# A hybrid attention/recurrence block on one core: VectorE, ScalarE and SP of the recurrence ordered by hand with a clock per engine

## The chip, the core and the metric

The kernel runs on one core of a Trainium2 chip. A core has a matrix engine (TensorE, PE in the profile; its weight loads are PEld), three elementwise engines (VectorE or DVE, ScalarE or ACT, GpSimd or POOL), a queue engine that issues transfers (SyncE or SP) and 16 DMA engines. Each engine takes its own instructions in a fixed order and waits at the head of that order for semaphores of the others. The metric is the device time of one execution in microseconds, as the median of several.

## What is computed

One block on 1024 tokens of width 1024, in float32. A projection of the normalized and modulated input feeds three branches: attention with a forget gate (8 heads of 64), a linear recurrence with a low-rank state update (RWKV-7, 8 heads of 64), and two sigmoid gates that mix the two. A feed-forward part with a short convolution follows. The recurrence, which the change is about:

```python
def step(state, inp):
    r_t, w_t, k_t, v_t, a_t, b_t = inp
    sa = jnp.einsum('bhvk,bhk->bhv', state, a_t)
    state = state * w_t[:, :, None, :] + sa[..., None] * b_t[:, :, None, :] + v_t[..., None] * k_t[:, :, None, :]
    y_t = jnp.einsum('bhvk,bhk->bhv', state, r_t)
    return state, y_t
_, y = lax.scan(step, state0, (tm(r_h), tm(w_h), tm(k_h), tm(v_h), tm(a_vec), tm(b_vec)))
```

Its output is normalized over each head, gets a bonus term `sum(r*k*r_k) * v`, and is multiplied by a gate.

## The kernel before

**Split products.** A float32 product is made from three products of rounded halves: an operand `x` is cast to `hi` (ScalarE) and `lo = x - hi` (VectorE), and PE adds `hi*hi + hi*lo + lo*hi`. So a tile of the projection (128 columns of `w_in`, one half of 512 tokens) is 24 matmuls into one PSUM bank, and each weight tile has a transfer on SP, a cast on ScalarE (line 272) and two subtractions on VectorE (line 274).

**Stages.** First the norms and the low-rank inputs, then the low-rank products (`lora_chain`), then the recurrence, attention, the branch and output products, and the feed-forward part. The stages overlap through one mechanism, the class `Weave`.

**Weave.** It keeps one number, `now`, an estimate of PE's time in ns, which every matmul advances by `mm_cost`. Python generators called chains emit instructions and yield the time that they want to wait. `run` always resumes the chain with the smallest rank whose time has come, and when none is due, `fill` emits matmuls from a queue of large tiles until one is: the tiles of q and k (`qk_steps`), of r, k, v of the recurrence (`rkv_items`), of the attention's v (`v_steps`) and of the 16 gates (`gate_steps`). So PE's order is written out by hand, chains and fill interleaved. The order on the other engines is not: the framework orders VectorE, ScalarE, GpSimd and SP in this stage with its own simulated timeline. What the recurrence has not used of the fill is run in attention, where a late form of the gates (`late_gate`, PSUM bank `rk_ps`) fills PE.

**The recurrence** works on 8 units: 4 pairs of heads times 2 halves of the sequence. A unit has 8 chunks of 64 tokens, and two heads side by side on the partitions. `pre_chain` runs `pre` for one unit after the other, `main_chain` runs `main` behind it.

- `pre` loads the decay and `a` (`cum`, `al`), scans, takes exponentials, normalizes the key (`head_sums`, line 686: a sum over each head as a product with a block matrix, of a high and a low half; the low half is a GpSimd subtraction, line 689), and makes the scaled operands `ar` and `bk`. PE forms their products per chunk (`p`, masked into `E` on line 758). The 32x32 diagonal blocks of `E` go through DRAM to another layout (`sm`, then `M32`; lines 766 and 770), 31 rows of an inverse are made there by pairs of small VectorE instructions (lines 778 and 780, 62 per unit), and the result returns through DRAM (`se`, then `TT`; lines 783 and 791). Meanwhile transposes (`vt`, `at`, `tb`) and a product `q` fill `UV`, `QA` and the third part of `E`.
- `main` completes the inverse (`X`, `xi`, `zi`), makes `Wt`, `Zt`, `Mt` and the parts of state and output that need no earlier state (`sp`, `yp`), and then steps through the chunks: a product of `Mt` and the state into `sp` and a scaling on VectorE into the next state `S` (line 897). Then comes the output: two more head sums (`mu`, `va`), the norm, the bonus and the gate.

**Waits in the order.** The points at which chains yield are fixed times found for this kernel (1150 ns between state steps, 2000 to 3400 ns at other places, 38500 ns for the inverse). The PSUM pool `gen` has four banks for the chains, `big` two for the fill.

**q, k and the heads of attention.** Each half tile of q or k is split and stored by six transfers of 64 rows into `d_st`, which holds for every head the stacked operands that attention multiplies (line 399). `load_head` (line 988) fetches a head by three GpSimd transfers, `stA`, `stB` and `vh`.

Of the kernel before, what the change touches and what calls it, by code (L numbers as in the profile page):

```python
# [9 lines left out]
F32 = mybir.dt.float32  # L10
# [6 lines left out]
S = 1024  # L17
# [26 lines left out]
NCST = _n  # L44
NC1 = 384
# [3 lines left out]
class Weave:  # L49
# [3 lines left out]
    def __init__(self):  # L53
        self.now = 0.0
        self.first = deque()
        self.queue = deque()
        self.cur = None
        self.loaded = deque()
        self.hold = 0.0
        self.clock = {}  # L60
        self.late = 0

# [22 lines left out]
    def step(self):  # L85

        while True:
            if self.cur is None:
# [4 lines left out]
                self.cur = run(w)  # L93
                self.prefetch()
            if next(self.cur, self) is not self:
                return True
            self.cur = None

# [14 lines left out]
    def spawn(self, chain, wait=0.0):  # L113

        self.live.append([self.now + wait, 0, chain])

    def run(self, chains):

        self.live = [[self.now, 1 + i, g] for i, g in enumerate(chains)]
        while self.live:  # L120
# [7 lines left out]
            else:  # L128
                due[0] = self.now + max(wait, 0.0)


@with_exitstack
def hybrid_block(ctx: ExitStack, tc: tile.TileContext, a, out):
# [70 lines left out]
    d_st = dr.tile([8, 4, 128, S], F32R, name="d_st")  # L204
# [50 lines left out]

    def load_w(src, name, pool=None, n=1024, scale=None, tags=("whi", "wlo"), bufs=2):

        pool = pool or wp
        raw = rp.tile([128, n], F32, tag="raw", name=f"raw_{name}")
# [5 lines left out]
        if weave.late == 1:  # L265
# [4 lines left out]
            weave.spawn(lower(9000), 0)  # L270
        else:
            nc.scalar.copy(hi, raw)  # L272
            for c in range(0, n, NH):
                nc.vector.tensor_tensor(lo[:, c : c + NH], raw[:, c : c + NH], f32(hi[:, c : c + NH]), op=ALU.subtract)  # L274
        return hi, lo
# [50 lines left out]

    def gate_steps(w, i, pps, ptag, pool, tag):
        if weave.late == 1:
            yield from late_gate(w, i)
            return  # L330
        for hf in range(2):
            cs = slice(hf * NH, hf * NH + NH)
            ps = pps.tile([128, NH], F32, tag=ptag, name=f"gt{i}_{hf}")
            yield from gemm_steps(ps, w, u, cs)

# [10 lines left out]
    with ExitStack() as es:  # L346
# [4 lines left out]
        def big(name):  # L351
            return pb.tile([128, NH], F32, tag="big", name=name)
# [4 lines left out]
        def shifted(w, ti, hf, dst, prev, name, by_kt=False):  # L357

            ps = big(f"ps_{name}{hf}")
            yield from gemm_steps(ps, w, u, slice(hf * NH, hf * NH + NH), by_kt=by_kt)  # L360
            sh = shp.tile([128, NH + 1], F32, tag="sh", name=f"sh_{name}{hf}")
# [7 lines left out]
            stt(dst, ps, omu[:, ti : ti + 1], sh[:, 0:NH], op0=ALU.mult, op1=ALU.add)  # L369

        rkv, got, last_col = {}, {}, {}

        def rkv_items(p, hf):
# [3 lines left out]
            def steps(w, x, t):  # L377
                if hf == 0:
                    last_col[p, x] = shp.tile([128, 1], F32, tag=f"pv{x}", name=f"pv{p}{x}")
                yield from shifted(w, t, hf, ts_[x], last_col[p, x], f"rkv{t}")  # L380
                got[p, hf] += 1
# [3 lines left out]

        def qk_steps(w, i):
            sc_ = 0.125 if i < 4 else 1.0
            for hf in range(2):
                cs = slice(hf * NH, hf * NH + NH)
                ps = big(f"qk{i}_{hf}")  # L390
                yield from gemm_steps(ps, w, u, cs)
                hi = gsp.tile([128, NH], F32R, tag="sp0", name=f"qh{i}_{hf}")
# [3 lines left out]
                h0 = 2 * (i % 4)  # L396
                for t, k, r0 in ((hi, 0, 0), (lo, 0, 64), (hi, 2, 0)) if i < 4 else ((hi, 1, 0), (hi, 1, 64), (lo, 3, 0)):
                    for h in range(2):
                        nc.sync.dma_start(f32(d_st[h0 + h, k, r0 : r0 + 64, cs]), f32(t[h * 64 : h * 64 + 64, :]))
# [157 lines left out]
        with tc.tile_pool(name="lg", bufs=1, reuse_waits="tile") as lg, \  # L557
# [65 lines left out]
            def forget():  # L623
# [10 lines left out]
                for hf in range(2):  # L634
# [28 lines left out]
                    nc.sync.dma_start(f32(d_st[:, 2, 64:68, cs]), f32(r[:, 0:4, :]))  # L663
                    nc.sync.dma_start(f32(d_st[:, 3, 64:68, cs]), f32(r[:, 2:6, :]))
# [21 lines left out]
        def head_sums(ps, x, hi, lo):  # L686

            nc.scalar.copy(hi, x)
# [1294 lines left out]
```

## Time and profile before

| | us |
|---|---|
| median of 3 runs (1680.43 to 1682.48) | 1680.87 |
| the profiled execution's own time | 1681.63 |
| its span in the trace | 1679.9 |
| granted TensorE clock, mean of the span | 0.993 |
| VectorE busy in the span | 1219.1 |
| ScalarE busy in the span | 806.3 |
| GpSimd busy in the span | 131.2 |

Views of the trace are read as follows. A row of a group names line, engine, operation, output and inputs by tile, shapes and count, then busy time and mean ns of one, then the idle time before them and what ended it. A row of waits names the waiting engine and tile, who released it, and total, number and longest. A row of the timeline begins with the start in us from the span's start and the length; in brackets stands the idle time before it. The window rows give busy time of every engine in a stretch. All matmuls have line 141 and all transposes line 145, since a helper records them, so they are told apart by tile. The end of a matmul is modelled, so the busy time of PE contains some waiting.

### The profile page before, as it was taken

The numbers are of one execution on the slowest core, as the hardware profiler recorded it, in microseconds if no ns is written. First come the engines' busy times: TensorE is split into PE (matmuls) and PEld (weight loads), VectorE is DVE, ScalarE is ACT, GpSimd is POOL, SyncE is SP. The second block draws the span as 40 slices with busy tenths as digits, with TensorE's granted clock in tenths as the row PEclk, the third lists the DMA queues.
The fourth block names the chain that finished last, engine by engine and source line by source line (L and its number), as shares of the span: only waits on it lengthen the run. The fifth ranks groups of instructions, "written<-read, shape, count | busy, mean of one in ns | idle before, by whom it ended". The sixth has DMA issues, their size and how long they took to land.

```text
span 1679.9 us, 26265 instructions
## 1 busy us (share of the span) xinstructions
PE 1630.3 (97%) x9870; PEld 1344.6 (80%) x9870; DVE 1219.1 (73%) x2402; ACT 806.3 (48%) x1481; POOL 131.2 (8%) x151
## 2 busy tenths in 40 slices
PE   7999999999999999999999999999999999999998
PEld 7777777787877778888878888888888888888886
DVE  5786787878866635888778455897777777786677
ACT  5563334434445446676633243654444444455455
POOL 0011001111111011212022000000000000000000
PEclk9999999999999999999999999999999999999999
DMA  8487644443332228434197420133322323584463
GB/s 332 143 322 233 181 124 123 130 120 98 100 112 88 89 67 202 126 108 128 35 335 262 177 88 38 63 120 111 109 95 94 119 95 107 182 276 152 130 211 108
DMA packets 121503, 240.79 MB, mean 143 GB/s; under 512 B 40032, under 2 KB 48608, under 8 KB 121376
## 3 DMA queue, kind: packets, MB, share of 16 engines
q1 hardware_dynamic: 112896, 220.74, 40.2%
q0 software_dynamic: 8480, 18.37, 4.3%
q8 instruction: 78, 1.28, 0.3%
q14 instruction: 49, 0.40, 0.1%
HBM read 173.51 MB, written 65.54 MB: 142 GB/s over the span
## 4 chain that ended last, share of the span: by engine, by line
PE 74%; DVE 14%; DMA 5%; ACT 3%; issue 2%; SPq 1%; DVEq 0%; ACTq 0%
PE X L141 13%; PE D L141 12%; PE Y L141 6%; PE wo L141 5%; PE ps_rkv L141 5%; PE br L141 5%; PE gt L141 4%; PE W L141 3%; PE rk_ps L141 3%; PE qk L141 2%; PE lg L141 2%; PE ov L141 2%; DVE E L780 2%; DVE t L778 2%; PE tr L141 2%
## 5 line engine op out<-in xcount | busy, mean ns | idle before, releaser
L141 PE MATMUL D<-op,op 128*128 128x512 f32 x924 | 209.8, 389 | 0.0
L141 PEld LDWEIGHTS D<-op,op 128*128 128x128 f32 x924 | 173.3, 188 | 36.3 <-DVE op L1246 0.3
L141 PE MATMUL X<-T_m,S 128*128 128x512 f32 x440 | 107.2, 390 | 0.2 <-ACT x L1522 0.2
L141 PEld LDWEIGHTS X<-T_m,S 128*128 128x128 f32 x440 | 82.4, 188 | 18.3 <-ACT x L1522 0.6
L1245 ACT CAST op<-g 128x512 fp32r<-128x512 f32 x77 | 47.8, 621 | 73.7 <-PE D L141 48.5
L1246 DVE TENSOR_TENSOR op<-g,op 128x512 fp32r<-128x512 f32 x77 | 53.0, 688 | 41.4 <-ACT op L1245 41.1
L1482 DVE SCALAR_TENSOR_TENSOR c<-ab,vec,c 128x512 f32<-128x512 f32 x88 | 65.9, 749 | 19.5 <-ACT c L1485 17.9
L778 DVE TENSOR_TENSOR t<-E,M 128x60 f32<-128x60 f32 (+24 forms) x248 | 57.6, 232 | 25.7 <-DMA M<-sm 20.3
L1446 DVE TENSOR_TENSOR S<-ur,S 128x512 fp32r<-128x512 f32 x66 | 45.5, 691 | 35.9 <-ACT S L1442 35.8
L1442 ACT CAST S<-ur 128x512 fp32r<-128x512 f32 x66 | 41.0, 622 | 55.8 <-DVE ur L1435 30.6
L1446 DVE TENSOR_TENSOR A<-ur,A 128x512 fp32r<-128x512 f32 x64 | 44.0, 688 | 30.9 <-ACT A L1442 30.7
L274 DVE TENSOR_TENSOR lo_in<-raw_in,hi_in 128x512 fp32r<-128x512 f32 x84 | 56.5, 712 | 12.5 <-PE gt L141 4.6
L141 PE MATMUL Y<-T_h,A 128*128 128x512 f32 x264 | 63.4, 389 | 0.0
L141 PE MATMUL Y<-T_h,S 128*128 128x512 f32 x264 | 63.3, 389 | 0.0
L272 ACT CAST hi_in<-raw_in 128x1024 fp32r<-128x1024 f32 x42 | 43.8, 1047 | 40.1 <-PE ps_rkv L141 23.2
L1048 ACT ACTIVATE P<-lg,nm 128x896 f32<-128x896 f32 (+3 forms) x64 | 47.5, 743 | 29.0 <-DVE nm L1044 20.8
L141 PE MATMUL X<-B_b,A 128*128 128x512 f32 x252 | 60.8, 390 | 0.0
L141 PE MATMUL W<-B_f,A 128*128 128x512 f32 x252 | 60.6, 389 | 0.0
L780 DVE TENSOR_TENSOR E<-E,t 128x60 f32<-128x60 f32 (+24 forms) x248 | 54.9, 221 | 5.7
L141 PEld LDWEIGHTS Y<-T_h,A 128*128 128x128 f32 x264 | 49.5, 188 | 10.4
L141 PEld LDWEIGHTS Y<-T_h,S 128*128 128x128 f32 x264 | 49.5, 188 | 10.3
L1442 ACT CAST A<-ur 128x512 fp32r<-128x512 f32 x64 | 39.9, 623 | 34.1 <-PE X L141 29.4
(475 smaller groups left out, 4130.9 us busy)
## 6 DMA issues: line engine op xcount, KB each, us to landing
raw_in<-in_w_in SPq DMA_DIRECT2D x50, 512.0 KB, 3.9
wm<-in_w_mod SPq DMA_DIRECT2D x48, 512.0 KB, 7.2
ur<-in_w_up SPq DMA_DIRECT2D x44, 512.0 KB, 4.2
g<-d_g SPq DMA_DIRECT2D x35, 512.0 KB, 4.1
d_g<-gs SPq DMA_DIRECT2D x44, 256.0 KB, 2.0
d_g<-c SPq DMA_DIRECT2D x33, 256.0 KB, 4.4
d_st<-qh SPq DMA_DIRECT2D x64, 128.0 KB, 2.4
stA<-d_st POOLq DMA_DIRECT2D x8, 1024.0 KB, 6.4
```

Source lines behind the costliest of these rows:

```text
L141: nc.tensor.matmul(o, lhsT, rhs, start=start, stop=stop, skip_group_check=more)
L272: nc.scalar.copy(hi, raw)
L274: nc.vector.tensor_tensor(lo[:, c : c + NH], raw[:, c : c + NH], f32(hi[:, c : c + NH]), op=ALU.subtract)
L778: tt(tv, E32[:, 0:J, s : s + 1].to_broadcast([128, J, W]), M32[:, s : s + 1, s + 1 : 32].to_broadcast([128, J, W]), op=ALU.mult)
L780: tt(E32[:, 0:J, s + 1 : 32], E32[:, 0:J, s + 1 : 32], tv, op=ALU.add)
L1048: nc.scalar.activation(e[:, 0:n], lg[:, 0:n], AF.Exp, bias=nm[:, 0:1], accum_out=nm[:, 1:2])
L1245: nc.scalar.copy(hi, src)
L1246: tt(lo, src, f32(hi), op=ALU.subtract)
L1442: nc.scalar.copy(hi, src)
L1446: tt(lo, src, f32(hi), op=ALU.subtract)
L1482: stt(c, ab[:, x + hf * NH : x + hf * NH + NH], V("conv_w", 22 * x + i), c, op0=ALU.mult, op1=ALU.add)
```

## The change

- In the recurrence VectorE, ScalarE and SP are put under the hand-made order as well: their instructions run in the order in which the program emits them.
- `Weave.on` is a clock for each engine. A chain asks for an engine with a cost in ns and a time from which its input is there, waits until the engine would be at most 250 ns from free, and gets the time at which the result is there (200 ns are added for the semaphore, 350 ns for a PSUM bank to drain, and 85 ns are taken off for the overlap of two instructions). All fixed waits of `pre` and `main` are replaced by such times.
- The fill's evacuations and weight splits become chains of their own (`evacuate`, `split_w`), spawned with rank 0 and 0.5. `room` and `ready_w` emit them at once where a bank or a weight is needed.
- The inverse rows become a chain (`solve`) of rank 1.5: behind `main` (1), ahead of `pre` (2).
- The four PSUM banks of the chains are handed out by `take` and `give`.
- The low halves of the head sums are VectorE subtractions (`halves_of`) and no longer on GpSimd.
- q and k are stored by kind (`d_qk`: q or k, high or low, 512 rows of all heads), two transfers of 128 rows per half tile. The forget sums go to `d_f`. `load_head` gathers a head by six transfers of 64 rows, two of four rows, and one for v.
- PE's cost model has other figures while the recurrence runs, among them 95 ns for a change between large and small matmuls.
- `run` ends with the two main chains and then emits what is left of the spawned ones; tiles beyond 12 left in the queue, if there are any, are run then, ahead of `load_head(0)`.

The core of the diff:

```diff
+LATENCY = 200.0
+DRAIN = 350.0
+OVERLAP = {"DVE": 85.0, "ACT": 85.0}
+AHEAD = 250.0
...
+    def on(self, engine, cost, after=0.0, ahead=AHEAD):
+        while not self.force:
+            wait = max(self.clock.get(engine, 0.0), after) - ahead - self.now
+            if wait <= 0:
+                break
+            yield wait
+        start = max(self.clock.get(engine, 0.0), after, self.now)
+        self.clock[engine] = start + cost - OVERLAP.get(engine, 0.0)
+        return start + cost + LATENCY
+
+    def through(self, chain):
+        self.force += 1
+        for _ in chain:
+            pass
+        self.force -= 1
...
+        if self.timed:
+            small = lhsT.shape[0] <= 64 or m <= 64
+            if small != self.small:
+                self.small = small
+                self.now += 95
+            if lhsT.dtype == F32R:
+                self.now += n / 2.2
+            else:
+                self.now += max(n, 50) * (0.87 if small else 1.74)
+            return
...
+    def split_w(hi, lo, raw, i):
+        while weave.worked < i - 1 and not weave.force:
+            yield 200
+        t = yield from weave.on("ACT", 1050)
+        nc.scalar.copy(hi, raw)
+        yield t - weave.now
+        for c in range(0, 1024, NH):
+            yield from weave.on("DVE", 700, t)
+            tt(lo[:, c : c + NH], raw[:, c : c + NH], f32(hi[:, c : c + NH]), op=ALU.subtract)
...
+    def room():
+        while len(outs) > 1:
+            weave.through(outs.popleft())
+
+    def evacuate(chain):
+        outs.append(chain)
+        weave.spawn(chain, DRAIN)
...
-                h0 = 2 * (i % 4)
-                for t, k, r0 in ((hi, 0, 0), (lo, 0, 64), (hi, 2, 0)) if i < 4 else ((hi, 1, 0), (hi, 1, 64), (lo, 3, 0)):
-                    for h in range(2):
-                        nc.sync.dma_start(f32(d_st[h0 + h, k, r0 : r0 + 64, cs]), f32(t[h * 64 : h * 64 + 64, :]))
+                for x, t in enumerate((hi, lo)):
+                    nc.sync.dma_start(f32(d_qk[i // 4][x][i % 4 * 128 : i % 4 * 128 + 128, cs]), f32(t))
...
-        def head_sums(ps, x, hi, lo):
-            nc.scalar.copy(hi, x)
-            nc.gpsimd.tensor_tensor(lo, x, f32(hi), op=ALU.subtract)
-            yield 3400
+        def halves_of(x, hi, lo, after=0.0):
+            t = yield from act(620, after)
+            nc.scalar.copy(hi, x)
+            t = yield from dve(690, t)
+            tt(lo, x, f32(hi), op=ALU.subtract)
+            return t
+
+        def head_sums(name, hi, lo, after):
+            yield after - weave.now
+            yield from take(1)
+            ps = gen(name)
             mm(ps, blk_r, hi, start=True, stop=False)
             mm(ps, blk_r, lo, start=False, stop=True)
+            return ps, weave.now + DRAIN
...
+        def solve(o, n, E, after):
+            sm = scr.tile([2, NCU, 2, 32, 32], F32, tag="sm", name=f"sm{n}")
...
+            after = t + 1800
+            while turn:
+                yield 200
+            turn.append(n)
...
+            after = t + 3500
+            t32 = rw.tile([128, 256], F32, tag="t32", name=f"t32{n}", bufs=1)
+            for s in range(31):
+                J, W = s // 4 + 1, 31 - s
+                tv = t32[:, 0 : J * W].rearrange("p (j w) -> p j w", w=W)
+                t = yield from weave.on("DVE", 220, after)
+                tt(tv, E32[:, 0:J, s : s + 1].to_broadcast([128, J, W]),
+                   M32[:, s : s + 1, s + 1 : 32].to_broadcast([128, J, W]), op=ALU.mult)
+                t = yield from weave.on("DVE", 220, t - LATENCY)
+                tt(E32[:, 0:J, s + 1 : 32], E32[:, 0:J, s + 1 : 32], tv, op=ALU.add)
+                after = t - LATENCY
...
+            o["ready"] = t + 2800
...
             for c in range(last_c + 1):
                 if S[c] is not None:
+                    yield t - weave.now
                     for h in range(2):
                         mm(sp[HS[h], c, :], Mt[HS[h], c, :], S[c][HS[h], :], start=False, stop=c == last_c, more=True)
                 S.append(rw.tile([128, CH], F32, tag="state", name=f"S{n}{c}", bufs=9))
-                marks["S"] = ts(S[-1], sp[:, c, :], pcd[:, c : c + 1], None, op0=ALU.mult)
-                if c + 1 < NCU:
-                    yield 1150
+                t = yield from dve(280, weave.now + DRAIN)
+                ts(S[-1], sp[:, c, :], pcd[:, c : c + 1], None, op0=ALU.mult)
...
-        weave.run([main_chain(), pre_chain()])
+        with tc.manual_schedule(engines={mybir.EngineType.SP, mybir.EngineType.DVE, mybir.EngineType.Activation}):
+            weave.timed = True
+            weave.run([main_chain(), pre_chain()])
+            while len(weave.queue) > 12:
+                weave.step()
+            weave.finish()
+            for x in (*outs, *splits):
+                weave.through(x)
+            weave.timed = False
...
-        nc.gpsimd.dma_start(A, d_st[h, 0:2, :, :].rearrange("k r s -> r k s"))
-        nc.gpsimd.dma_start(B[0:68, :, :], d_st[h, 2:4, 0:68, :].rearrange("k r s -> r k s"))
+        hs = slice(h * 64, h * 64 + 64)
+        for t, rs, k, x in ((A, 0, 0, 0), (A, 0, 1, 0), (A, 64, 0, 1), (A, 64, 1, 0), (B, 0, 0, 0), (B, 0, 1, 1)):
+            nc.gpsimd.dma_start(t[rs : rs + 64, k, :], d_qk[k][x][hs, :])
+        for k in range(2):
+            nc.gpsimd.dma_start(B[64:68, k, :], d_f[h, 2 * k : 2 * k + 4, :])
```

`take(n)` yields until n of the four `gen` banks are given back and then until the latest of their times; `give(t)` returns a bank as free from t.

More of the change, by code (lines that the diff above doesn't have):

```diff
@@ L684, in hybrid_block, with take, give, dve @@
         nc.gpsimd.dma_start(blk_r, a["cst"][:, NC2 : NC2 + 128].bitcast(F32R))
-        def head_sums(ps, x, hi, lo):
-            nc.scalar.copy(hi, x)
-            nc.gpsimd.tensor_tensor(lo, x, f32(hi), op=ALU.subtract)
-            yield 3400
+        free = deque([0.0] * 4)
+        def take(n):
+            while len(free) < n:
+                yield 100
+            yield max(free.popleft() for _ in range(n)) - weave.now
+        def give(t):
+            free.append(t)
+        def dve(cost, after=0.0):
+            return weave.on("DVE", cost, after)
@@ L750, in pre @@
             UV = chunk_tile("UV", 2, NCU, 2, CH)
+            made = []
             for c0 in range(0, NCU, 4):
+                yield from take(2)
                 ps = [gen(f"p1_{n}{h}{c0}") for h in range(2)]
@@ L795, in pre @@
+            rkb = tmp("ksq")
+            t_rkb = yield from dve(745)
+            stt(rkb, rr, V("r_k", p), al, op0=ALU.mult, op1=ALU.mult)
+            yield from take(2)
             vt, at = gen(f"vt{n}"), gen(f"at{n}")
```

381 lines of the change are left out of this document (275 added, 106 removed).

## The prediction

> **What bounds the kernel now.** The page gives the profiled execution's span, the busy shares, and the count of engines that could be the limit.
>
> ```profile
> span 1679.9 us, 26265 instructions
> PE 1630.3 (97%) x9870; PEld 1344.6 (80%) x9870; DVE 1219.1 (73%) x2402; ACT 806.3 (48%) x1481; POOL 131.2 (8%) x151
> ```
>
> TensorE (PE) is busy for 97%, so a change that adds and removes no large matmuls can only win what is left of its idle time. The next view, the busy time by stretch, says where that is. I cut at the end of the low-rank stage (141.45), at the last lone matmuls ahead of attention (643.8) and at the first branch matmul (842.16). Columns: stretch, its length, busy time of PE, PEld, DVE, ACT, POOL, granted clock, DMA share, GB/s.
>
> ```profile
> 141.45:643.80 502.35, 484.86 (x4379) 389.62 (x4378) 346.67 (x972) 218.48 (x385) 67.03 (x87) 1.00 0.44 123
> 643.80:842.16 198.36, 189.57 (x1176) 164.94 (x1176) 163.51 (x331) 134.16 (x307) 30.24 (x35) 1.00 0.40 110
> 842.16:1679.90 837.74, 828.17 (x3700) 684.74 (x3700) 609.58 (x943) 377.36 (x674) 23.80 (x16) 0.99 0.42 143
> ```
>
> PE is idle 17.5 us in the recurrence, 8.8 in attention, 9.6 after it. VectorE is at 69% in the recurrence: not the limit of the stage. The waits of PE in that first stretch (waiter, releaser, total, times, longest) name the 17.5:
>
> ```profile
> PE sp L141 <- DVE S L897: 5.1, 8, 1.2
> PE q L141 <- DVE QA L805: 3.5, 2, 3.2
> PE qk L141 <- DVE v L369: 2.8, 1, 2.8
> PE uw L141 <- ACT TT L853: 1.8, 1, 1.8
> PE p L141 <- DVE bk L738: 0.8, 1, 0.8
> ```
>
> They are 14.0 us, all on VectorE or ScalarE work that came later than PE's fixed order supposed. The timeline of the longest, PE's row, VectorE's rows behind it, and the four microseconds of clock after it:
>
> ```profile
> 475.63 1.15 PE L141 MATMUL q<-UV,E 64*64 64x64 f32 x32 [3.25 <-DVE QA L805]
> ...
> 471.87 0.43 DVE L836 STREAM_TRANSPOSE X<-TT 32x256 f32<-32x256 f32 x1 [4.71 <-DMA TT<-se]
> 473.29 0.43 DVE L836 STREAM_TRANSPOSE X<-TT 32x256 f32<-32x256 f32 x1 [0.98 <-DMA TT<-se]
> 473.75 1.73 DVE L805 COPY QA<-at 64x256 f32<-64x256 f32 x4
> ...
> 476.00:480.00 4.00, 4.00 (x35) 3.28 (x31) 0.20 (x1) 3.15 (x6) 1.27 (x1) 0.61 0.49 135
> ```
>
> `X` of one unit waited for its transfer, `QA` of the next unit stood behind it on VectorE, and PE stood behind `QA` though fill was at hand. The stall cost 3.25 us and then a granted clock of 0.61 for 4 us, worth 0.39 x 4 = 1.6 us: 4.8 together. So the stage's own loss is 17.5 + 1.6 = 19.1 us.
>
> PE is not out of work there. The gate products are the last of the fill:
>
> ```profile
> L141 PE MATMUL gt<-u_hi,hi_in 128*128 128x512 f32 x144 | 40.5, 411 | 0.0
> 141.45 10.24 PE qk L141 x45
> ```
>
> Eight matmuls of this kind belong to one half tile: 144/8 = 18 halves, nine of the 16 gates. Seven are left for attention. A dense fill matmul takes 10.24/45 = 0.228 us, so a gate of 48 is 10.9 us of PE wherever it runs.
>
> **The change part by part.** *The order by hand.* VectorE, ScalarE and SP now issue in the order of the Python program, at times that a clock per engine foretells, and PE's pieces are placed by the same clocks. No arithmetic goes. Its worth is the share of the 19.1 us that was mis-foretold. The clocks' figures are near the rows: 690 ns for a 512-column tensor_tensor, 220 for a solver step, 280 for a state step, against
>
> ```profile
> L737 DVE TENSOR_TENSOR al<-al,k 128x512 f32<-128x512 f32 x8 | 5.5, 684 | 0.0
> L780 DVE TENSOR_TENSOR E<-E,t 128x60 f32<-128x60 f32 x24 | 5.2, 218 | 0.6
> L897 DVE TENSOR_SCALAR S<-sp,pcd 128x64 f32<-128x64 f32 x60 | 16.8, 280 | 26.1 <-PE sp L141 25.9
> 409.45 0.68 DVE L733 TENSOR_TENSOR bk<-kr,en 128x512 f32<-128x512 f32 x1
> 410.05 0.54 DVE L736 TENSOR_SCALAR al<-al,vec,oka 128x512 f32<-128x512 f32 x1
> ```
>
> and the 85 ns of overlap that they deduct shows as well: the second of two starts 0.60 after the first, which lasts 0.68. I take two thirds of the loss as recovered, 12.7 us. Upper bound: all 19.1. Lower bound: below nothing, since another stage whose VectorE and ScalarE already stand in a hand-made order, attention, idles 8.79/198.36 = 4.4% against 17.49/502.35 = 3.5% here; at 4.4% the stage would lose 22.3 us, 4.8 more than now. I go nearer to the upper end because attention's VectorE is at 82% and this stage's at 69%.
>
> *The state steps.* They are seven or eight per unit, and their pace now:
>
> ```profile
> 407.02 0.33 PE L141 MATMUL sp<-S,Mt 64*64 64x64 f32 x4
> 407.28 1.66 PE L141 MATMUL ps_rkv<-u_lo,hi_in 128*128 128x512 f32 x6
> 408.87 0.33 PE L141 MATMUL sp<-S,Mt 64*64 64x64 f32 x4
> ```
>
> One step per 1.85 us, with six fill matmuls in it. By the new clocks a step can follow after 0.35 + 0.28 + 0.20 = 0.83 us plus its own 0.26, some 1.1 us. Over 7 steps and 8 units that is about 40 us of chain, which is not 40 us of time: less fill is run meanwhile, about 3.7 gates, and attention runs them instead. Price nothing, as long as attention has room: its VectorE would have four instructions of some 0.684 us more per gate, 10 us in all, in a stage that is 40 us longer. If the room is not there, it costs part of that, which is in the range.
>
> *No GpSimd halves.* Four low halves per unit go from GpSimd to VectorE.
>
> ```profile
> L689 POOL TENSOR_TENSOR en<-ksq,cum 128x512 fp32r<-128x512 f32 x8 | 12.3, 1540 | 33.6 <-ACT cum L688 33.6
> L689 POOL TENSOR_TENSOR Mtr<-y,Ztr 128x512 fp32r<-128x512 f32 x8 | 10.3, 1290 | 113.6 <-ACT Ztr L688 113.6
> ```
>
> 32 instructions of 0.684 us are 21.9 us of VectorE, 19.2 at the spacing of 0.60: 366 to 369 of 502 us, 73%. Each head sum comes 0.6 to 0.9 us earlier (1.29 to 1.54 against 0.68). On the path: nothing, hidden by PE's fill; uncovered it would be those 19 to 22 us.
>
> *The inverse rows as a chain.* The 62 solver instructions per unit get a rank below the main chain, so `S`, `QA` and evacuations go between them. These stalls of VectorE on transfers are what it can avoid:
>
> ```profile
> DVE t L778 <- DMA M<-sm: 20.3, 7, 6.0
> DVE X L836 <- DMA TT<-se: 14.6, 5, 5.1
> ...
> DMA to landing us min/median/max: 2.2/2.7/5.4
> ```
>
> It allows 3.5 us for `M`, whose landing has a median of 2.7 and a maximum of 5.4. So a late one still blocks VectorE for up to 1.9 us, less than a 24-matmul tile of fill (5.5 us). Its share of the gain is in the 12.7.
>
> *q and k by kind.* 96 stores of 128 KB become 32 of 256 KB, and a head is loaded by nine transfers in place of three.
>
> ```profile
> L399 SPq DMA_DIRECT2D d_st<-qh x64: 445/595/1696, 133.3 to 304.5; - x64
> L990 POOL DMA_DIRECT2D stA<-d_st x8: 696/702/742, 627.5 to 779.0; - x8
> L992 POOL DMA_DIRECT2D stB<-d_st x8: 993/993/1001, 628.2 to 779.7; - x8
> stB<-d_st POOLq DMA_DIRECT2D x8, 544.0 KB, 14.0
> ```
>
> SP is spared 64 x 0.595 = 38 us of issuing, ahead of which the loads of `cum`, `al` and weights stood. GpSimd issues eight in place of two: 5.6 to 7.9 us against 1.7, per head. stA's issues lie (779.0 - 627.5)/7 = 21.6 us apart; 5.6 of issuing and 14.0 of landing fit in that, 7.9 and 14.0 miss it by 0.3, on seven heads 2 us. Uncovered whole, the 4 to 6 us more of issuing cost 28 to 42 us; spared waits of SP are worth 0 to 2.8 (the `qk` wait). I take nothing for both.
>
> Sum: 12.7 us off the profiled execution's 1681.6 (span 1679.9 and 1.7 around it) gives 1668.9; the median of the runs is 0.8 below that execution, so 1668.2.
>
> **The rivals.** *More than the idle time.* All 19.1 us go, the two `p` pieces of a unit are issued together (eight switches fewer; the fill row above spends 1.59 - 6 x 0.228 = 0.22 on its two switches, so 1.8 us), and attention, with four more gates to fill with, loses half of its 8.8: 25.3 us, 1655.6. For: the fill is there. Against: attention's waits are inside its own chains.
> The Trainium skill (Perfetto Trace Analysis, Identifying the Most-Contended Engine) says that matmul busy time misjudges headroom, since matmuls are pipelined, and weight-load busy time is to be used. By it the stage is at 77.6% and the stage after attention at 81.7%; at that share the recurrence would take 476.9 us, a gain of 25.5 and 1655.4. The trace agrees that PE's busy time hides some loss (the 0.22 above); small matmuls with short weight loads spoil the ratio.
>
> *The stage idles like attention* (the change does not do what it says). The hand order is no better than the other hand-ordered stage: 4.4% idle, 4.8 us more, 1685.7. For: that row. Against: VectorE's lower share.
>
> *VectorE stands behind a late transfer in every unit.* Now nothing reorders: when `M`, `TT` or `cum` lands late, all that is queued behind on VectorE waits, PE behind it, and the clock falls. A stall like the one at 475 costs 4.8 us; in all eight units 38.8 on top of the 1668.2: 1707. It turns the sign from the third stall on. For: landing reaches 5.4 against 3.5 allowed. Against: a store of 5.5 us of fill and two large PSUM banks lie between VectorE and PE, and at this length the stall came once in eight units.
>
> **How the numbers follow.** Forecast 0.55, at 1668.2, its own range 1662 to 1676; more 0.16; like attention 0.15, of which over half is within 0.2% (0.2% is 3.4 us, about what measurement can tell); late transfers 0.14. Faster 0.71, same 0.08, slower 0.21. The range from 1653, just under the rival with more, to 1693, five late transfers, leaves out under 2 in 10.
>
> **What would show it.** Right: the five waits of PE quoted above fall from 14.0 us to under 5; no clock under 0.95 there; state steps at 1.0 to 1.3 us; fewer than nine gates done ahead of attention, whose stretch is longer by their 10.9 us each; POOL's four rows gone; stA landing ahead of its first `lg`. Wrong: waits of PE on VectorE work that itself waited for `M`, `TT` or `cum`; PE short of fill in attention; `lg` waiting for a head.

## The result and the profile after

The changed kernel takes 1709.09 us (median of 4 runs, 1703.28 to 1714.03) against 1680.86 for the kernel before: a ratio of 1.0165, 95% interval 1.0131 to 1.0199. It is slower by some 28 us, outside the predicted range of 1653 to 1693.

The page of the changed kernel, first lines:

```profile
span 1708.7 us, 26206 instructions
PE 1642.7 (96%) x9870; PEld 1354.0 (79%) x9870; DVE 1237.0 (72%) x2434; ACT 810.8 (47%) x1477; POOL 102.0 (6%) x163
```

The span is 28.8 us longer with the same 9870 matmuls. Where the 28.8 lie is told by the busy time by stretch. Both kernels are now cut at marks that exist in both: 142, the first gate matmul that runs inside attention (tile `rk_ps`), and the first branch matmul (`br`). Columns as in the prediction's window rows. The kernel before:

```profile
142.00:636.75 494.75, 478.67 (x4353) 384.89 (x4352) 345.46 (x971) 214.97 (x378) 65.08 (x85) 1.00 0.43 120
636.75:842.16 205.41, 195.21 (x1201) 169.25 (x1200) 164.21 (x332) 137.67 (x313) 31.94 (x38) 1.00 0.43 115
```

and the kernel after:

```profile
142.00:669.68 527.68, 519.48 (x4538) 417.29 (x4537) 367.14 (x1018) 237.54 (x412) 20.56 (x54) 0.99 0.39 115
669.68:869.69 200.01, 167.84 (x1008) 147.56 (x1008) 155.74 (x316) 118.99 (x273) 46.25 (x78) 0.92 0.44 97
869.69:1708.70 839.01, 828.15 (x3700) 684.51 (x3700) 611.06 (x943) 377.28 (x674) 22.41 (x16) 0.99 0.42 143
```

Two things are to be seen. The recurrence is 32.9 us longer, but PE is idle in it for only 8.2 us instead of 16.1: it is longer because 185 more matmuls run in it. Attention is only 5.4 us shorter although 193 matmuls fewer run in it; PE idles there for 32.2 us instead of 10.2, and the granted clock is 0.92 instead of 1.00. The matmuls that moved are gates. A group of PE in the changed kernel (busy time, mean ns), and the row of one form of the late gates in attention (ns min/median/max, first and last start):

```profile
L186 PE MATMUL gt<-u_lo,hi_in 128*128 128x512 f32 x208 | 56.0, 399 | 0.0
```

```profile
L186 PE MATMUL rk_ps<-u_hi,lo_in x48: 387/390/476, 673.1 to 744.1; 128*128 128x512 f32 x48
```

Eight matmuls of a form are half a gate, so 208/16 = 13 gates run ahead of attention and 48/16 = 3 in it; before they were nine and seven. At the prediction's 10.9 us per gate, four gates are 43.8 us, and the balance is:

- recurrence: 527.7 - 43.8 = 483.9 without the four gates, against 494.75: 10.9 us won in this reckoning, which takes a gate's whole length off (run with nine gates, it takes 504.0: e6 below);
- attention: 205.4 - 43.8 = 161.6 were to be expected with three gates, 200.0 were taken: 38.4 us lost, 22.0 of them more PE idle, the rest a longer busy time of the matmuls that stayed, at a granted clock of 0.92 (0.08 x 167.8 = 13.4 us);
- after attention: 1.3 us lost. Together 28.8.

The waits of PE in the recurrence (waiter, releaser, total, times, longest), the whole list:

```profile
PE p L186 <- DVE bk L971: 5.9, 3, 3.2
PE ps_rkv L186 <- ACT hi_in L309: 1.2, 1, 1.2
PE qk L186 <- DVE ql L517: 0.8, 1, 0.8
PE ps_rkv L186 <- DVE lo_in L313: 0.2, 1, 0.2
```

Four of the five waits that the prediction quoted are gone; the fifth, `p`, has grown from 0.8 to 5.9 us. In attention the list begins:

```profile
PE ov L186 <- DVE o L1411: 16.4, 11, 2.4
PE ov L186 <- DVE tl L1378: 6.7, 6, 1.6
PE lg L186 <- ACT P L1342: 2.2, 4, 1.5
```

These are attention's own chains on VectorE and ScalarE. Before, gate matmuls ran in their gaps; now the last of them starts at 744.1, and from there on nothing is left to run:

```profile
760.00:800.00 40.00, 30.48 (x193) 27.33 (x194) 32.71 (x66) 21.16 (x49) 12.91 (x21) 0.91 0.50 94
800.00:840.00 40.00, 30.12 (x188) 26.55 (x187) 31.13 (x66) 21.96 (x54) 9.28 (x14) 0.87 0.32 67
840.00:880.00 40.00, 32.89 (x159) 27.98 (x158) 25.78 (x50) 20.02 (x43) 2.66 (x3) 0.83 0.34 117
```

Why did the recurrence use four gates more? Because its own chain of work became longer, and `fill` covers whatever the chain leaves open. The tile `X` opens the main chain of every unit; its rows (count, ns min/median/max, first and last start) give the pace of the units, first before, then after:

```profile
L836 DVE STREAM_TRANSPOSE X<-TT x16: 422/434/437, 222.3 to 577.7; 32x256 f32<-32x256 f32 x16
```

```profile
L1090 DVE STREAM_TRANSPOSE X<-TT x16: 422/434/436, 216.6 to 621.0; 32x256 f32<-32x256 f32 x16
```

From the first to the last there are seven steps: 355.4 us before, some 50.8 each, and 404.4 after, some 57.8 each. The timeline after shows what VectorE lacks. PE's runs of `uw` and `mz`, and the rows of the inverse of another unit (lines 885 and 888) beside them; in brackets the idle time ahead of a row:

```profile
343.97 1.96 PE L186 MATMUL uw<-QA,TT 64*64 64x128 f32 x32
349.26 1.96 PE L186 MATMUL mz<-E,Wt 64*64 64x128 f32 x32
...
343.68 0.19 DVE L885 TENSOR_TENSOR t<-E,M 128x28 f32<-128x28 f32 x1
345.11 0.42 DVE L1121 COPY Wt<-uw 128x256 f32<-128x256 f32 x1 [1.24 <-PE uw L186]
345.98 0.42 DVE L1121 COPY Wt<-uw 128x256 f32<-128x256 f32 x1 [0.45 <-PE uw L186]
346.32 0.18 DVE L888 TENSOR_TENSOR E<-E,t 128x28 f32<-128x28 f32 x1
...
348.61 0.21 DVE L885 TENSOR_TENSOR t<-E,M 128x50 f32<-128x50 f32 x1
350.40 0.42 DVE L1149 TENSOR_TENSOR Mt<-cst,mz 128x256 f32<-128x256 f32 x1 [1.58 <-PE mz L186]
```

The row after that of 343.68 needs nothing but VectorE's own result. It comes 2.6 us later all the same, behind the copies of `uw`, because in the order written out it stands behind them. The program explains it: a chain is resumed only where the running one yields, or between fill matmuls. While the main chain emits the 32 matmuls of `uw` no other chain is asked, and an engine is given work at most 250 ns ahead of `now`; so VectorE has nothing until the matmuls end. The waits of VectorE in the recurrence show the sum of it:

```profile
DVE Mt L1149 <- PE mz L186: 19.4, 16, 3.5
...
DVE Wt L1121 <- PE uw L186: 11.7, 15, 2.1
...
DVE cum L934 <- DMA cum<-d_lora: 4.9, 2, 4.0
```

31.1 us ahead of these two evacuations alone. Before, where the framework ordered VectorE, `Mt` is not in the list and `Wt` stands with less:

```profile
DVE Wt L864 <- PE uw L141: 3.3, 2, 2.9
```

In sum VectorE idles about as large a share of the stretch as before (160.5 of 527.7 us, 149.3 of 494.75, 30% both): the waits on the transfers of `M` and `TT`, 34.9 us before, are nearly gone, and these came in their place.

### The profile page after: what moved, and what is told of

It is laid out like the page before. It is cut to its first block, busy times and chain, and to the rows that moved or that the text cites. A ratio compares the mean times of both kernels' runs of the same rounds, so it can differ in the third digit from the quotient of the medians.

```text
span 1708.7 us, 26206 instructions
## 1 busy us (share of the span) xinstructions
PE 1642.7 (96%) x9870; PEld 1354.0 (79%) x9870; DVE 1237.0 (72%) x2434; ACT 810.8 (47%) x1477; POOL 102.0 (6%) x163
## 4 chain that ended last, share of the span: by engine, by line
PE 79%; DVE 8%; ACT 2%; DMA 1%; issue 1%; SPq 0%; POOL 0%; ACTq 0%; DVEq 0%
PE X L186 13%; PE D L186 12%; PE gt L186 8%; PE Y L186 6%; PE wo L186 5%; PE ps_rkv L186 5%; PE br L186 5%; PE qk L186 3%; PE W L186 3%; PE v L186 3%; PE ov L186 2%; DVE nm L1338 2%; PE rk_ps L186 2%; PE lg L186 2%; PE sp L186 1%; PE tp L190 1%
## 5 line engine op out<-in xcount | busy, mean ns | idle before, releaser
L309 ACT CAST hi_in<-raw_in 128x1024 fp32r<-128x1024 f32 x38 | 39.7, 1044 | 43.9 <-DMA raw_in<-in_w_in 40.5
L186 PE MATMUL ov<-th,vh 128*128 128x256 f32 (+1 forms) x160 | 42.5, 313 | 17.6 <-DVE o L1411 16.4
L186 PEld LDWEIGHTS Y<-T_h,A 128*128 128x128 f32 x264 | 49.6, 188 | 10.4
L1378 DVE TENSOR_TENSOR tl<-tp,th 128x512 fp32r<-128x512 f32 (+1 forms) x80 | 49.9, 633 | 10.6 <-ACT th L1375 10.1
L885 DVE TENSOR_TENSOR t<-E,M 128x60 f32<-128x60 f32 (+24 forms) x248 | 51.8, 209 | 6.6 <-DMA M<-sm 0.7
L1375 ACT CAST th<-tp 128x512 fp32r<-128x512 f32 (+1 forms) x80 | 42.8, 542 | 28.5 <-PE tp L190 27.9
```

The source lines that it names most:

```text
L186: nc.tensor.matmul(o, lhsT, rhs, start=start, stop=stop, skip_group_check=more)
L885: tt(tv, E32[:, 0:J, s : s + 1].to_broadcast([128, J, W]), M32[:, s : s + 1, s + 1 : 32].to_broadcast([128, J, W]), op=ALU.mult)
L1375: nc.scalar.copy(th[:, 0:w], tp[:, 0:w])
L1378: tt(tl[:, 0:w], tp[:, 0:w], f32(th[:, 0:w]), op=ALU.subtract)
```

## The experiments

All ratios are against the kernel before, with runs of it on the same chip. "Gates" is how many of the 16 run ahead of attention and in it.

| | what | us | ratio, interval | gates |
|---|---|---|---|---|
| e1 | before, attention left three gates | 1718.3 | 1.0233, 1.0212 to 1.0254 | 13 + 3 |
| e2 | after, chains resumed inside a chain's matmuls | 1681.8 | 1.0013, 0.9997 to 1.003 | 9 + 7 |
| e3 | after, halves on GpSimd | 1701.9 | 1.014, 1.0115 to 1.0164 | 12 + 4 |
| e4 | after, q and k stacked by head | 1712.6 | 1.0204, 1.0182 to 1.0226 | 13 + 3 |
| e5 | e2 with a longer lead for `pre` | 1698.1 | 1.0098, 1.0085 to 1.0111 | 9 + 7 |
| e6 | after, nine gates at most in the recurrence | 1693.8 | 1.0075, 1.006 to 1.009 | 9 + 7 |
| e7 | before, halves on VectorE | 1682.1 | 1.0008, 0.9995 to 1.002 | 9 + 7 |
| e8 | before, q and k by kind | 1672.1 | 0.9947, 0.9932 to 0.9962 | 9 + 7 |
| e9 | before, e7 and e8 together | 1671.8 | 0.9958, 0.9945 to 0.9972 | 9 + 7 |
| e10 | after, inverse rows ahead of both chains | 1738.3 | 1.0343, 1.0313 to 1.0374 | 15 + 1 |
| e11 | after, only small chains resumed | 1701.9 | 1.0136, 1.0114 to 1.0159 | 12 + 4 |

**e1: is it the gates that attention lacks?** The kernel before, with four gates more run between the last unit and attention:

```diff
-            while len(weave.queue) > 12:
+            while len(weave.queue) > 2:
```

> The kernel before with one constant changed: at the end of the recurrence the queue of gates is run down to two (and the one already loaded), so attention has 3 gates to fill with, as in the changed kernel, and not 7. Theory A (attention runs dry of fill): four gates of 10.9 us run ahead of attention, and attention hardly gets shorter because its own chains on VectorE and ScalarE set its length: 1681 + 44 - 5 = 1720, between 1710 and 1725, attention about 200 us with 25 to 35 us of PE idle time. Rival B (attention of the changed kernel is slow for its head loads by kind on GpSimd): attention shrinks by the 44 us and the time stays at 1681 to 1687.

1718.3, as the theory had it. No order of any engine was changed, only where four gates run:

```profile
142.00:682.07 540.07, 523.73 (x4543) 421.61 (x4542) 356.66 (x986) 238.59 (x414) 65.01 (x86) 0.99 0.44 124
682.07:875.71 193.64, 161.45 (x1009) 141.40 (x1008) 153.28 (x316) 118.52 (x273) 26.22 (x32) 0.96 0.28 82
```

The first stretch grows by 45.3 us, about four gates, and attention shrinks by 11.8 only. That is 33.5 us for four gates: a gate moved out of attention here costs 8.4 of its 10.9 us.

**e2: is it that chains are not resumed?** In the changed kernel, after every matmul that a chain emits, other chains whose time has come are resumed:

```diff
+    def poll(self):
+        while True:
+            due = min((c for c in self.live if c[0] <= self.now and not any(c is x for x in self.active)),
+                      key=lambda c: (c[1], c[0]), default=None)
+            if due is None:
+                return
+            self.resume(due)
...
         nc.tensor.matmul(o, lhsT, rhs, start=start, stop=stop, skip_group_check=more)
+        if weave.timed and weave.active and not weave.force:
+            weave.poll()
```

> The changed kernel, but while a chain emits a run of matmuls without a pause, the other chains that have come due are resumed after each matmul, so that VectorE, ScalarE and SP are given work during the runs of PE. Same instructions, same costs and ranks. Theory A (in the plan the units stand 58 us apart because nothing is given to VectorE during some 12 us per unit of such runs): the plan's last output comes 43 us sooner than the changed kernel's (574 against 617), about four gates move back into attention, its PE idle time falls under 12 us: 1664 to 1676, units about 51 us apart. Rival B (head loads): attention stays at 25 to 32 us idle, 1700 or more. Rival C (the halves load VectorE too much): units stay at 57 us or more, 1700 or more.

1681.8, outside the theory's 1664 to 1676: the mechanism is the one named, but the gain over the kernel before did not come, and the units start 53.8 us apart (`X` from 211.5 to 588.2), not 51. Windows and VectorE's waits of this run:

```profile
142.00:636.73 494.73, 484.34 (x4354) 387.03 (x4353) 360.29 (x1005) 215.25 (x377) 21.24 (x58) 1.00 0.39 115
636.73:841.81 205.08, 195.05 (x1202) 169.29 (x1200) 163.91 (x332) 137.92 (x313) 49.79 (x81) 1.00 0.48 113
```

```profile
DVE Wt L1141 <- PE uw L202: 5.1, 5, 1.6
...
DVE Mt L1169 <- PE mz L202: 3.2, 2, 2.7
```

The waits ahead of `uw` and `mz` fall from 31.1 to 8.3 us, the gates are again nine and seven, and attention is 205.1 us as before, at a clock of 1.00. PE idles 10.4 us in the recurrence, and yet it is as long as before the change, 494.7: PE is busy in it for 5.7 us more. That 142 falls at another point of the run-in is not the reason: from the span's start to the first attention gate PE is busy for 612.3 us against 606.9 before. What keeps the same matmuls busy for longer is not settled.

**e3 and e4: the change without one part.** The low halves back on GpSimd, planned at 1400 ns:

```diff
-            t = yield from dve(690, t)
-            tt(lo, x, f32(hi), op=ALU.subtract)
+            t = yield from weave.on("POOL", 1400, t)
+            nc.gpsimd.tensor_tensor(lo, x, f32(hi), op=ALU.subtract)
```

> The changed kernel with the low halves of the head sums back on GpSimd (at 1400 ns in the plan). Theory A: the plan's last output comes 13 us sooner (604 against 617), one gate more in attention: 1692 to 1704. Rival C (these 32 instructions on VectorE are the loss): back to 1685 or less. Rival B: unchanged, 1705 to 1712.

1701.9, one gate fewer. Then q and k stored and loaded as before:

```diff
-            for x, y in enumerate((hi, lo)):
-                yield from weave.on("SP", 450, t if x else 0.0)
-                nc.sync.dma_start(f32(d_qk[i // 4][x][i % 4 * 128 : i % 4 * 128 + 128, cs]), f32(y))
+            h0 = 2 * (i % 4)
+            for y, k, r0 in ((hi, 0, 0), (hi, 2, 0), (lo, 0, 64)) if i < 4 else ((hi, 1, 0), (hi, 1, 64), (lo, 3, 0)):
+                for h in range(2):
+                    yield from weave.on("SP", 450, t if y is lo else 0.0)
+                    nc.sync.dma_start(f32(d_st[h0 + h, k, r0 : r0 + 64, cs]), f32(y[h * 64 : h * 64 + 64, :]))
```

> The changed kernel with q and k stored and loaded as before: six stores of 128 KB per half tile, three transfers per head. Theory A: the plan's last output is where it was (618 against 617), attention just as dry: 1703 to 1713. Rival B (nine transfers per head on GpSimd delay attention): 1678 to 1692.

1712.6, with 13 gates as in the change. Neither part is the loss. By the gates the halves carry one of the four; the times differ by 7.2 us from the change for the halves and by 3.5 for storing by kind, and in both cases the intervals overlap. Attention takes 199.6 us with the loads as before, 200.0 in the change: the loads by kind are not what makes it long.

**e5: a better plan?** e2, with every VectorE request of `pre` made 300 ns ahead in place of 250, and the nine gates fixed:

```diff
-            yield from dve(745)
+            yield from weave.on("DVE", 745, 0.0, 300)
...
-            while len(weave.queue) > 12:
+            while len(weave.queue) > 6:
```

> The changed kernel with chains resumed also between a chain's own matmuls, with the products' chain (pre) asking VectorE 300 ns ahead instead of 250 (before the inverse rows' 250), and with nine gate tiles kept in the recurrence and seven for attention. The plan's own clock puts its last output 24 us earlier than in the run with resuming alone, about two of which are not gate work. Theory A (the chain was starved by the rows; once it isn't, what is left is PE work): at most the 10.4 us of PE idle that the run with resuming alone still had in the recurrence can be won, more likely 2 to 7 us: 1674 to 1681 us, first attention gate at 630 to 636 us. Rival B (resuming alone had already found the bound): 1680 to 1684. Rival C (pre now delays the rows and so the state steps): above 1690.

1698.1, where the third reading had been "above 1690":

```profile
142.00:646.77 504.77, 482.80 (x4349) 386.75 (x4347) 357.89 (x1003) 216.40 (x380) 25.01 (x64) 0.99 0.41 117
```

PE idles 22.0 us with the same gates, and the stretch is 10 us longer than in e2; attention is longer by 8 (213.1 us). Yet the chip followed the plan: the last output of the recurrence is stored at 612.5, against 634.0 in e2, 21.5 us earlier where the plan's clock had 24, and the units start 50.8 us apart (`X` from 217.2 to 572.8). So the rows and state steps were not held up on the whole; the third reading had the number, not the cause. What is left of the nine gates then runs by itself: from 612.5 to the first gate of attention PE is busy for 26.5 of 34.3 us, waiting 3.4 for a gate's evacuation on VectorE and 4.3 for a weight's cast on ScalarE. The other 14.2 us of idle lie ahead of 612.5, where e2 has 10.4 up to its last store.

**e6: are the four gates the length, or only the filling?** The changed kernel, TensorE idling where the recurrence would take a tenth gate:

```diff
+                if self.timed and self.loaded[0][2] and len(self.queue) <= 6:
+                    return False
```

> The changed kernel, but the recurrence may use nine gate tiles only (as before the change) and TensorE idles where it would have used more; seven are left to attention. Theory A (the recurrence's length is set by its planned chains, and its extra gates only fill the holes): the recurrence stays 515 to 530 us long from 142 (first attention gate at 655 to 672) with 35 us or more of PE idle in it, attention is 203 to 208 us again, and the time is 1695 to 1718. Rival B (the recurrence is bound by PE work, and the four gates are what makes it longer): first attention gate at 625 to 640, time 1665 to 1680.

```profile
142.00:645.98 503.98, 480.40 (x4352) 386.82 (x4351) 356.26 (x1002) 215.43 (x379) 22.57 (x59) 0.97 0.39 113
645.98:854.23 208.25, 198.22 (x1201) 172.00 (x1199) 165.38 (x334) 136.81 (x311) 48.75 (x78) 0.98 0.49 112
608.00:645.98 37.98, 23.09 (x281) 18.41 (x280) 14.85 (x41) 11.71 (x23) 6.71 (x12) 0.69 0.33 75
```

1693.8, between the two readings. The limit takes hold only in the last unit: up to 608 PE is busy as in the changed kernel (457.3 us from 142 on, 457.8 there), and the units start 57.7 us apart as there (`X` from 217.4 to 621.2). Of the four gates' 43.8 us, 23.7 leave the stretch with them (527.7 to 504.0), behind the last `X`: the last unit's output is stored at 649.9 instead of 666.6, since without fill in between its chain is resumed sooner. The rest stays, as 15.4 us more idle than in the changed kernel, mostly. So in the last unit the plan's holes are real, and filling them with gates lengthens it further; for the units ahead of it this run shows nothing. And with nine gates this recurrence is 9.2 us longer than before the change, not 10.9 shorter.

**e7 to e9: the other parts alone, on the kernel before.** The halves on VectorE:

```diff
-            nc.gpsimd.tensor_tensor(lo, x, f32(hi), op=ALU.subtract)
+            tt(lo, x, f32(hi), op=ALU.subtract)
```

> The kernel before, with the low halves of the recurrence on VectorE instead of GpSimd and nothing else changed; its waits between steps are fixed numbers, so the plan doesn't change. Theory A (the halves cost VectorE nothing in the recurrence; in the changed kernel they cost only through its plan): 1677 to 1684. Rival B (32 subtractions more on VectorE lie on the path by themselves): 1686 to 1702. Rival C (the sooner halves shorten PE's waits): 1668 to 1676.

No difference (1682.1). The stores and loads by kind, as in the change:

```diff
-                for t, k, r0 in ((hi, 0, 0), (lo, 0, 64), (hi, 2, 0)) if i < 4 else ((hi, 1, 0), (hi, 1, 64), (lo, 3, 0)):
-                    for h in range(2):
-                        nc.sync.dma_start(f32(d_st[h0 + h, k, r0 : r0 + 64, cs]), f32(t[h * 64 : h * 64 + 64, :]))
+                for x, t in enumerate((hi, lo)):
+                    nc.sync.dma_start(f32(d_qk[i // 4][x][i % 4 * 128 : i % 4 * 128 + 128, cs]), f32(t))
```

> The kernel before, with q and k stored by kind and each head loaded in eight pieces, nothing else changed. Theory A (nothing on the path): 1677 to 1684. Rival B (the head's pieces land late for the logits, or GpSimd's issuing delays its halves): 1686 or more. Rival C (SP spared of its issues shortens a wait in the recurrence): 1670 to 1676.

1672.1: rival C. The recurrence and the whole list of its PE waits:

```profile
142.00:628.28 486.28, 477.33 (x4353) 384.75 (x4352) 344.48 (x971) 215.35 (x378) 66.20 (x92) 1.00 0.39 114
```

```profile
PE sp L141 <- DVE S L895: 4.7, 6, 1.0
PE q L141 <- DVE QA L803: 2.2, 2, 2.0
PE v L141 <- DVE vs L948: 0.9, 1, 0.9
PE mz L141 <- ACT E L810: 0.5, 1, 0.5
PE v L141 <- DVE v L370: 0.3, 1, 0.3
```

8.5 us come out of the recurrence, 7.1 of them PE idle (16.1 to 8.95). The `qk`, `uw` and `p` waits that I had put down to VectorE's order are gone without an order by hand. SP's own timeline in the first unit shows a part of the reason, before and then in e8, with the rows of `X` in e8 behind it:

```profile
168.58 1.73 SPq L399 DMA_DIRECT2D d_st<-qh  x3
170.41 1.19 SPq L399 DMA_DIRECT2D d_st<-ql  x2
171.64 0.60 SPq L399 DMA_DIRECT2D d_st<-qh  x1
172.34 2.04 SPq L766 DMA_DIRECT2D sm<-E  x4
```

```profile
169.10 1.83 SPq L764 DMA_DIRECT2D sm<-E  x4
```

```profile
L834 DVE STREAM_TRANSPOSE X<-TT x16: 422/435/439, 215.2 to 569.1; 32x256 f32<-32x256 f32 x16
```

The first transfer of the inverse is issued 3.2 us later before than in e8: for 1.1 us of that its input `E` came later, and for some 2 it stood behind the six stores of q and k. `X` of the first unit comes at 215.2 instead of 222.3, and of the last at 569.1 instead of 577.7: 7.1 of the 8.6 us are won in the first unit, where the stores are densest, and the pace after that is the same, 50.6 against 50.8. How much of the gain is SP's issuing, this run doesn't separate: storing by kind also writes a third fewer bytes (32 x 256 KB for 96 x 128 KB, since one half of each tile was stored twice), and the framework, which orders VectorE here, chose another order (`QA` from `q` stands behind the first pair of the inverse's rows before, behind the third in e8). Both parts together:

> The kernel before with q and k by kind and with the low halves on VectorE: all of the change but the order by hand and the rows as a chain of their own. Theory A (the two parts add: by kind 9.6 us less, halves 0.3 us more, each measured alone on the kernel before): 1669 to 1677. Rival B (by kind gained because GpSimd was short, so that it gains nothing once the halves are gone): 1679 to 1684.

1671.8: they add. This kernel, like e8, beats both the kernel before and the changed one. The order by hand with all that belongs to it (the rows, evacuations and splits as chains, the handing out of banks, PE's cost model) is then what stands between 0.9958 and 1.0165, a ratio of 1.0208, some 35 us.

**e10 and e11: which chain is starved?** The inverse rows ahead of both other chains:

```diff
-            weave.spawn(solve(o, n, E, t), 0, 1.5)
+            weave.spawn(solve(o, n, E, t), 0, 0.7)
```

> The changed kernel with the inverse rows ahead of both other chains, so that they give way to none. By the plan's own clock the last output comes 17.6 us later, 1.6 gate tiles more. Theory A (what is lost is that a chain is not resumed while another emits TensorE work, whichever gives way): 14 or 15 gates used ahead of attention, 1711 to 1735. Rival B (that the rows give way, and come late, is the loss): the recurrence is shorter, 1680 to 1700.

1738.3, a little over the theory's range, with 240/16 = 15 gates gone ahead of attention. So it is not the giving way that loses. And e2's resuming, with the two long chains left out of it:

```diff
-            due = min((c for c in self.live if c[0] <= self.now and not any(c is x for x in self.active)),
+            due = min((c for c in self.live if c[0] <= self.now and c[1] not in (1, 2)),
```

> The changed kernel with only the rows, the splits and the evacuations resumed between a chain's own matmuls, not the two main chains themselves. By the plan's own clock the last output comes 10.6 us sooner than in the changed kernel, one gate tile fewer; with all chains resumed it was 43 us and four gates. Theory A (the two main chains starve each other, so that resuming the small ones alone mends a quarter): 12 gates ahead of attention, 1693 to 1705. Rival B (VectorE's rows alone were starved): nine gates, 1676 to 1688.

1701.9, 12 gates: by the gates a quarter of what full resuming mends, as expected (the interval overlaps that of the change). The two long chains hold up each other, not only the rows.

## Why the prediction was wrong

**The step that failed** stands under the state steps: "less fill is run meanwhile, about 3.7 gates, and attention runs them instead. Price nothing, as long as attention has room". The sign of the gates was wrong, and with it the price. I looked at the main chain's state steps and took the recurrence's chain to become shorter. What sets the pace of the units is the circle of `pre`, the rows and `main` through VectorE, and in the written order that circle grew from 50.8 to 57.8 us per unit. Four gates more were run in place of 3.7 fewer, and attention, which I had only asked whether it has room for more, ran short: 38.4 us by the balance above, and e1 shows most of it, 32.0 us (attention 193.6 where 161.6 were to be expected), with nothing but the gates moved. The other 6.4 us are not explained; the granted clock of attention is 0.92 in the changed kernel and 0.96 in e1. That the circle grew because chains are not resumed is shown by e2, where resuming brings back the four gates and 4.0 of the 7.0 us per unit (53.8). "PE short of fill in attention" stood among the signs of a wrong prediction; it had no chance and no price, though the row of attention (VectorE at 82%, PE filled by seven gates) was on the table.

**The order by hand: 12.7 us.** The 10.9 us of the balance come near it by luck: they take four gates off at full length, and the recurrence that really runs nine (e6) is 9.2 us longer than before. With resuming mended and the gates at nine (e2), the order by hand leaves as much PE idle (10.4) as the framework's order does in e9's recurrence (9.6):

```profile
142.00:629.00 487.00, 477.36 (x4353) 384.67 (x4352) 350.37 (x1003) 215.35 (x378) 23.54 (x59) 1.00 0.40 116
```

e9 has the change's other two parts as e2 has them, and its recurrence is 7.7 us shorter than e2's, nearly all of it PE's busy time. The two ratios, 1.0013 and 0.9958, have intervals that lie apart: even mended, the order by hand loses some 9 us to the framework's.

Five waits "on VectorE or ScalarE work that came later than PE's fixed order supposed" was a true reading of the releasers, but not the end of it: three of them (`qk`, `uw` and `p`, 5.4 of the 14.0 us) go when q and k are stored by kind, with no order by hand (e8); most of `sp` and `q` stays (4.7 and 2.2 us).

**q and k by kind: "I take nothing for both".** On the kernel before it is worth 9.6 us (e8); in the changed kernel 3.5 by the medians, which is not clear of noise (e4). The 38 us of SP's issuing were too few, since the stores that are left are issued faster too (64 at 595 and 32 at 558 ns before, 32 at 320 in e8: some 46 us), and they were then bounded by the one `qk` wait, 2.8. The head's loads did stay hidden, as priced: no `lg` of the changed kernel waits for a transfer.

**No GpSimd halves: nothing.** Right for the part by itself (e7 and e9). In the written order it costs one gate; the 7 us between e3 and the change are not clear of noise.

**The state steps.** The pace of 1.1 us wasn't reached, as fill still goes between. In the changed kernel they start 2.5 and 1.4 us apart here:

```profile
415.82 0.33 PE L186 MATMUL sp<-S,Mt 64*64 64x64 f32 x4
...
418.35 0.33 PE L186 MATMUL sp<-S,Mt 64*64 64x64 f32 x4
...
419.74 0.33 PE L186 MATMUL sp<-S,Mt 64*64 64x64 f32 x4
```

**The rivals.** None came about. Late transfers did not stand in VectorE's way: where `M` and `TT` cost it 20.3 and 14.6 us before, the loads of `cum` with 4.9 are the largest wait on a transfer in the recurrence now. Nor does the recurrence idle like attention: 8.2 of 527.7 us are 1.6%. The missing rival was the plan itself: an order can be kept to the letter by the chip, with almost no idle PE, and be the wrong order, since the fill that hides its holes is taken from the next stage.

## What to carry to other kernels

Where a stage fills its gaps from a store of work that a later stage lives on too, its busy share says nothing of how good its order is: count what it draws from the store, and price one item of it in the later stage (here 8 to 10 us of each gate's 10.9). An order written by one thread of a program is given away to other engines only where that thread looks up; every run of instructions without such a point is idle time planned for all engines that others should have fed. A wait's releaser is not its cause: follow it once more, down to the queue that issued its data.

## What was not expected of the hardware

PE's granted clock in the dry part of attention falls to 0.91, 0.87 and 0.83 over 40 us each, although no single wait of PE there is longer than 2.4 us: many short gaps (30.5 us busy of 40) went with it. They don't always: a stretch of attention in e1, with 29.2 us busy and no wait longer than 2.2, has the full clock.

```profile
800.00:840.00 40.00, 29.23 (x207) 25.88 (x207) 35.49 (x75) 24.62 (x59) 6.70 (x8) 1.00 0.36 105
```

The Trainium skill (TensorE: Matmul & The Clock Gate, A second HAM failure mode: psum-queue depth-cycling) says that frequent short idle spells between groups of matmuls made the clock swing in one kernel; the windows of the changed kernel agree, that of e1 does not. The same page of the Trainium skill, in Part 1: The HAM clock gate, gives an idle window of about 3.4 us as what turns the clock down; here the clock fell where no wait was as long. Together with the idle time itself the lower clock made the four gates moved out of attention cost 33.5 (e1) to 38.4 us of their 43.8. In e6, whose waits reach 7.4 us, 14.9 of the 23.6 us of idle lie in the last 38 us of the recurrence, and the granted clock is 0.69 there.

And SP's queue: two stores of 256 KB in place of six of 128 KB took 8.5 us out of the recurrence of the kernel before, with some 46 us less of issuing and a third fewer bytes. In the first unit a small transfer, on which VectorE and then PE wait, stood some 2 us behind such stores; how much of the 8.5 comes from issuing is not shown.
